# Output matmuls of a pair issued ahead of a later pair's scores, transposes behind them, in an encoder trunk

## The chip, the core and the metric

The kernel runs on one core of one Trainium2 chip, as one launch with everything in 32-bit floats. The metric is the device time of one execution in microseconds (us). Times of the kernel before: 1628.23, 1629.42 and 1628.72, median 1628.72.

The engines are named as the profile names them: PE (TensorE, matmuls), DVE (VectorE), ACT (ScalarE), POOL (GpSimd) and SP (SyncE, which only issues DMAs here). Each works through a queue of its own, in an order fixed when the program is built, and waits on semaphores for the others.

## The reference

Two sequences of 256 tokens with 1024 features go through two layers that share their weights between the sequences. Cut to what matters here:

```python
h = rmsnorm(x, attn_norm[l])
a_cols, b_cols, c_cols, d_cols, g_cols = split(h @ w_in[l])
o_a = diff_mixer(a_cols)     # 4 heads, two softmaxes of 32-row heads, their difference
o_b = natten_mixer(b_cols)   # 4 heads of 64, neighbourhood mask and a position bias b_rpb
o_c = mla_mixer(c_cols)      # low-rank queries and keys, 96 rows a head
o_d = gqa_mixer(d_cols)      # 4 query heads of 64, 2 key heads, rotary in two axes
merged = sum(sigmoid(g_cols_i) * (o_i @ w_branch[l, i]))
x = x + merged @ w_out[l]
x = x + conv_ffn(rmsnorm(x, ffn_norm[l]))      # gated, width 2816, 3-tap conv
...
y = rmsnorm(x, final_norm)                     # after both layers
```

In each mixer `softmax(q k^T) v` is taken per head over the 256 keys of the own sequence.

## The kernel before

**Pieces and units.** Both sequences lie side by side as T = 512 columns, the features on the partitions, so a projection is a sum of matmuls with a 128x128 weight block and 512 columns of activations. The weights are read once, in a fixed order, as pieces of mostly 128 x 1024 values (512 KB). SP loads piece by piece into three `raw` buffers (`load_piece`, L267). Each is split into a rounded high part and the rest (`split_piece`, L278): ACT writes `wh` (L288), then DVE the first half of `wl` (L291) and POOL the second (L292). Every product is three matmuls, `wh` by `xh`, `wh` by `xl` and `wl` by `xh` (`mm3`, L296 to L298), so that a piece of 8 blocks gives 24 matmuls. The work on one piece is a unit. The program's units follow the order of the pieces: queries and keys of mixer b (units 1 to 4, `psbq` and `psbk`), values of b (`psvb`), then mixers a, d and c, then gates `pg` with branch products `pb`, output projection, and the MLP. Projections land in four PSUM banks in turn; a bank comes free when its evacuation has read it.

**Side work.** Everything that isn't a projection is written as generators that are handed from unit to unit. Those of the diff and of the prediction:

- `pair_gen` (L811): attention of two heads for one sequence. Scores `sc` of the pair (L744; for mixers a, b and d interleaved on parts of the array, `scores_rows`), softmax of the first head, softmax of the second, then two groups of four transposes (`pt`, L787), each copied to SBUF by ACT as `ptr` (L793); then the output matmuls `po` (L842, four calls that the trace shows as eight matmuls; the two heads use the two halves of 64 columns of the array), and their evacuation. TLAG and PLAG are numbers of extra steps ahead of the transposes and ahead of `po`, for each mixer.
- `sq_gen` (L1154): the squares of x for the first normalisation, added up by `sq_acc` (squares on ACT; additions on DVE, L338).
- `norm_gen`: the statistics matmuls `st` (L344, columns of one element), then the mean square `ms` and a newton iteration for 1/sqrt on DVE (L306 to L352, ending in the copy `rs`), then four transposes that broadcast it (`rb`, L357), the copy `rsrow` (L372), and on POOL the rotary tables times that row (`cosr`, `sinr`, L379 and L380). Projections run on unnormalised x; their evacuation multiplies by `rsrow` (`bc`, L601, for `psbq` and `psbk`).
- `bias_gen` (L698): 16 DMAs of the position bias on SP's queue (L695), then on POOL four additions of the mask (L704).
- `lam_gen`: the scalars `lam` of mixer a on DVE (L1173 to L1179).

**Order.** The loop from L1185 goes over the units. At the start of a unit every active generator takes one step, in the order of priority and, within one, in the order in which they were added. Then come the unit's own matmuls, one more step of the generators (`vec(0)`, `vec(1)`) with the evacuations that are due, the split of the piece two units on, and the load of the piece five units on. `sq_gen` is added in unit 0 and yields twice; `norm_gen` and `bias_gen` are added in later units. What is written in this order then passes a scheduler of the framework, which fixes the order on each engine when the program is built: it may put an instruction past others on its engine. What stands in the program is therefore read from the order of the built program, not from the loop alone.

**Buffers in PSUM.** The banks are four for projections (two of the scores of mixer a take theirs there too), two for scores, one for the transposes `pt`, and one that `po`, `st` and `rb` share.

Of the kernel before, what the change touches and what calls it, by code (L numbers as in the profile page):

```python
# [32 lines left out]
GX = [(25, 29), (31, 32)]  # L33
GBR = {n: n - BLAG for n in range(BLAG, 30)} | {30: 29, 31: 30}
TLAG = {"a": 1, "b": 1, "c": 0, "d": 0}
PLAG = {"a": 2, "b": 0, "c": 1, "d": 2}
GAP = {"a": 3, "b": 2, "c": 2, "d": 3}
START = {"a": ("ak0", 7), "b": ("bk0", 4), "c": ("cv", 6), "d": ("vf1", 2)}
CLAG = 1
# [162 lines left out]
def trunk_kernel(ctx: ExitStack, tc: tile.TileContext, xt, wflat, gains, lams, rpb, consts, yt):  # L202
# [22 lines left out]
    def psum(nm, pool=pm):  # L225
        tag = {id(pm): "m", id(psx): "s", id(pst): "t", id(pso): "o"}[id(pool)]
        return pool.tile([128, T], F32, tag=tag, name=nm)
# [7 lines left out]
    def rows64(ap):  # L235
        return ap.rearrange("p (r c) -> p r c", c=64)
# [30 lines left out]
    def load_piece(i, parts=1):  # L267
        if i >= len(order):
            return
        n = _piece_cols(order[i][1])  # L270
        raw = wpool.tile([128, 1280], F32, tag="raw", name=f"raw{i}", bufs=RAW_BUFS)
        src = wflat[offs[i]:offs[i] + 128 * n].rearrange("(p n) -> p n", p=128)
        c = n // parts
        for q in range(parts):
            nc.sync.dma_start(out=raw[:, q * c:q * c + c], in_=src[:, q * c:q * c + c])
        raws[i] = raw
# [23 lines left out]
    def split(v, h, l, eng=None):  # L300
        S.activation(out=h, in_=v, func=AF.Copy)  # L301
        (eng or V).tensor_tensor(out=l, in0=v, in1=f(h), op=ALU.subtract)  # L302
# [132 lines left out]
    def build_layer(l):  # L435
# [271 lines left out]
        def heads(mix, j):  # L707
            if mix == "a":
                return [[(f"aq{j}", f"ak{j}", 32 * (2 * e + c), 32) for c in range(2)] for e in range(2)]
            if mix == "b":  # L710
                return [[(f"bq{j}", f"bk{j}", 64 * e, 64)] for e in range(2)]
            if mix == "c":
                return [[(f"cq{2 * j + e}", f"ck{2 * j + e}", 0, 96)] for e in range(2)]
            return [[(f"dq{j}", "dk", 64 * e, 64)] for e in range(2)]
# [3 lines left out]
        def scores(maps, b):  # L718
            out = []
            for qn, kn, p0, n in maps:  # L720
                ps = psum("sc", psx)
                (qh, ql), (kh, kl) = att[qn], att[kn]
                ks = slice(b * 256, b * 256 + 256)
                p = slice(p0, p0 + n)
                for qt in range(2):
                    qs = slice(b * 256 + qt * 128, b * 256 + qt * 128 + 128)
                    o = ps[:, qt * 256:qt * 256 + 256]
                    PE.matmul(o, lhsT=qh[p, qs], rhs=kh[p, ks], start=True, stop=False)
                    PE.matmul(o, lhsT=qh[p, qs], rhs=kl[p, ks], start=False, stop=False)
                    PE.matmul(o, lhsT=ql[p, qs], rhs=kh[p, ks], start=False, stop=True)  # L730
                out.append(ps)
            return out

        def scores_rows(maps, b):
            pss = [psum("sc", psx if i < 2 else pm) for i in range(len(maps))]
            ks = slice(b * 256, b * 256 + 256)
            for qt in range(2):
                qs = slice(b * 256 + qt * 128, b * 256 + qt * 128 + 128)
                for term in range(3):
                    for ps, (qn, kn, p0, n) in zip(pss, maps):  # L740
                        p = slice(p0, p0 + n)
                        q = att[qn][1 if term == 2 else 0]
                        k = att[kn][1 if term == 1 else 0]
                        PE.matmul(ps[:, qt * 256:qt * 256 + 256], lhsT=q[p, qs], rhs=k[p, ks],  # L744
                                  start=(term == 0), stop=(term == 2))
            return pss
# [36 lines left out]
        def trans(p):  # L783
            ps = psum("pt", pst)
            for kt in range(2):
                for qt in range(2):
                    PE.transpose(out=ps[:, kt * 256 + qt * 128:kt * 256 + qt * 128 + 128],  # L787
                                 in_=p[:, qt * 256 + kt * 128:qt * 256 + kt * 128 + 128], identity=ident)
            return ps

        def trans_evac(ps):
            t = t2("ptr")
            S.activation(out=t, in_=ps, func=AF.Copy)  # L793
            return t

        def v_of(mix, j, e, tt):
            if mix == "a":
                return vA[:, tt, (2 * j + e) * 64:(2 * j + e) * 64 + 64]
            if mix == "b":
                return vB[:, tt, (2 * j + e) * 64:(2 * j + e) * 64 + 64]  # L800
            if mix == "c":
                return vC[:, tt, (2 * j + e) * 64:(2 * j + e) * 64 + 64]
            return vD[:, tt, e * 64:e * 64 + 64]

        def o_tile(mix, j, part, dt):
            key = ("o", mix, j, part)
            if key not in att:
                att[key] = t2(f"o{mix}{j}{part}", dt)
            return att[key]

        def pair_gen(mix, b, j):  # L811
            hs = heads(mix, j)
            rows = mix in "abd"
            if rows:
                ss = scores_rows(hs[0] + hs[1], b)
                s0, s1 = ss[:len(ss) // 2], ss[len(ss) // 2:]
            else:
                s0 = scores(hs[0], b)
            yield
            p0 = softmax(mix, j, 0, s0)  # L820
            yield
            if not rows:
                s1 = scores(hs[1], b)
            yield
            p1 = softmax(mix, j, 1, s1)
            yield
            for _ in range(TLAG[mix]):
                yield
            t0 = trans(p0)
            yield  # L830
            pt0 = trans_evac(t0)
            yield
            t1 = trans(p1)
            yield
            pt1 = trans_evac(t1)
            yield
            for _ in range(PLAG[mix]):
                yield
            ops = psum("po", pso)
            for kt in range(2):  # L840
                for e, pt in ((0, pt0), (1, pt1)):
                    PE.matmul(ops[64 * e:64 * e + 64, :256], lhsT=v_of(mix, j, e, 2 * b + kt),  # L842
                              rhs=pt[:, kt * 256:kt * 256 + 256], start=(kt == 0), stop=(kt == 1))
            yield
            bs = slice(b * 256, b * 256 + 256)
            if mix == "a":
                S.activation(out=o_tile("a", j, "f", F32)[:, bs], in_=ops[:, :256], func=AF.Copy)
            else:
                h, lo = o_tile(mix, j, "h", F32R), o_tile(mix, j, "l", F32R)
                if mix == "b":  # L850
                    split(rows64(ops[:, :256])[:, :, ::-1], rows64(h[:, bs]), rows64(lo[:, bs]))
                else:
                    split(ops[:, :256], h[:, bs], lo[:, bs])
            yield
# [34 lines left out]
        def at(step, gen, pri=1):  # L889
            starts.setdefault(step, []).append((pri, gen))  # L890
# [198 lines left out]
        for mix in ORD:  # L1089
# [6 lines left out]
            if mix == "a":  # L1096
                at(s - GAP[mix] + 4 + (TLAG["a"] + PLAG["a"] + 1) // 2, a_norm_gen)
        tabs = row_tables()
# [83 lines left out]

    units[3]["side"].append((1, lam_gen))

    active, pending = [], []  # L1185
    for i, u in enumerate(units):
        active += [(pri, g()) for pri, g in u["side"]]
        active.sort(key=lambda a: a[0])
        live = []
        for pri, g in active:  # L1190
            if next(g, 1) is None:
                live.append((pri, g))
        active = live
        wh, wl = splits.pop(i)
        u["pe"](wh, wl)

        def vec(want):
            for a in list(active):
                if a[0] == want:
                    if next(a[1], 1) is not None:  # L1200
                        active.remove(a)

        vec(0)
        now = [e for e in pending if e[0] <= i]
        pending = [e for e in pending if e[0] > i]
        for _, e in now:
            e()
        vec(1)
        split_piece(i + LOOK)
        load_piece(i + LOOK + RAW_BUFS)  # L1210
        if u["now"] and u["evac"] is not None:
            u["evac"]()
        elif u["evac"] is not None:
            pending.append((max(i + 1, u["nb"]), u["evac"]))
# [58 lines left out]
```

## Time and profile before

| what | value |
|---|---|
| median of 3 runs | 1628.72 us |
| the profiled execution, its own time | 1629.04 us |
| its span in the trace | 1627.3 us |
| PE busy | 1610.2 us, 99% of the span, 8163 matmuls |
| DVE busy | 962.9 us, 59% |
| ACT busy | 620.5 us, 38% |
| POOL busy | 661.2 us, 41% |
| DMA | 146.84 MB on SP's queue, 26.8% of the 16 DMA engines' span |
| mean granted clock of PE | 0.995 of full speed |

The span is the part of the execution that the trace covers; the 1.7 us around it belong to the execution's own time. PE's busy share is that of its matmuls with modelled ends: they overlap, and where PE is never idle a stretch is read by the steps from one matmul's start to the next. In the chain that ended last PE holds 97%, DVE and ACT 1% each.

### The profile page before, as it was taken

How to read it: one execution, taken by the hardware profiler on the slowest of the kernel's cores; microseconds unless marked ns; L12 is line 12 of the kernel's file. 1: busy time of each engine (PE TensorE's matmuls, PEld its weight loads, DVE VectorE, ACT ScalarE, POOL GpSimd, SP SyncE). 2: the span in 40 equal slices, each digit the busy share in tenths (PEclk: the TensorE clock that was granted, in tenths of full speed). 3: DMA queues.
4: the chain of work that ended last, by engine and by line, in shares of the span. 5: the costliest groups of instructions: out<-in, count | busy, mean ns of one | idle time of the engine just before them, and what ended most of it. 6: DMA issues, size and time to landing. Idle time of an engine off the chain costs nothing.

```text
span 1627.3 us, 21327 instructions
## 1 busy us (share of the span) xinstructions
PE 1610.2 (99%) x8163; PEld 1336.7 (82%) x8163; DVE 962.9 (59%) x1580; ACT 620.5 (38%) x1107; POOL 661.2 (41%) x449
## 2 busy tenths in 40 slices
PE   8999999999999999999999999999999999999997
PEld 6898788888888888888888977888788888888886
DVE  7767485656876665633366665756468656665113
ACT  4446354333333333322234555434332333333221
POOL 4432223445534444444445231244455344444342
PEclk9999999999999999999999999999999999999999
DMA  6213122221322322223332222222222222322331
GB/s 220 101 53 98 56 98 82 81 78 59 116 91 91 104 95 98 90 95 105 102 105 85 67 88 72 82 86 76 81 78 104 92 95 99 104 91 86 105 96 64
DMA packets 50534, 149.25 MB, mean 92 GB/s; under 512 B 13184, under 2 KB 16128, under 8 KB 50432
## 3 DMA queue, kind: packets, MB, share of 16 engines
q1 hardware_dynamic: 49344, 146.84, 26.8%
q8 instruction: 64, 1.05, 0.3%
q10 hardware_dynamic: 1088, 1.05, 0.2%
q14 instruction: 38, 0.31, 0.1%
HBM read 145.77 MB, written 2.10 MB: 91 GB/s over the span
## 4 chain that ended last, share of the span: by engine, by line
PE 97%; DVE 1%; ACT 1%; issue 1%; DMA 0%; POOL 0%; SPq 0%; POOLq 0%; ACTq 0%
PE pf L296 10%; PE pf L297 10%; PE pf L298 10%; PE pg L296 7%; PE pg L297 7%; PE pg L298 7%; PE pfo L296 5%; PE pfo L297 5%; PE pfo L298 5%; PE po L842 2%; PE pt L787 2%; PE pb L298 2%; PE pwo L296 2%; PE pb L297 2%; PE pb L296 2%; PE pwo L298 2%
## 5 line engine op out<-in xcount | busy, mean ns | idle before, releaser
L292 POOL TENSOR_TENSOR wl<-raw,wh 128x512 fp32r<-128x512 f32 (+4 forms) x264 | 454.4, 1723 | 567.6 <-ACT wh L288 466.6
L288 ACT ACTIVATE wh<-raw 128x1024 fp32r<-128x1024 f32 (+5 forms) x264 | 281.6, 1067 | 437.4 <-PE pfo L297 128.2
L291 DVE TENSOR_TENSOR wl<-raw,wh 128x512 fp32r<-128x512 f32 (+4 forms) x262 | 258.9, 988 | 227.6 <-ACT wh L288 209.8
L296 PE MATMUL pf<-xh,wh 128*128 128x512 f32 x704 | 274.3, 390 | 0.0
L298 PE MATMUL pf<-xh,wl 128*128 128x512 f32 x704 | 273.9, 389 | 0.0
L297 PE MATMUL pf<-xl,wh 128*128 128x512 f32 x704 | 273.9, 389 | 0.0
L296 PE MATMUL pg<-xh,wh 128*128 128x512 f32 x512 | 203.4, 397 | 0.4
L297 PE MATMUL pg<-xl,wh 128*128 128x512 f32 x512 | 199.7, 390 | 0.0
L298 PE MATMUL pg<-xh,wl 128*128 128x512 f32 x512 | 199.7, 390 | 0.0
L296 PEld LDWEIGHTS pf<-xh,wh 128*128 128x128 f32 x704 | 132.2, 188 | 27.4
L298 PEld LDWEIGHTS pf<-xh,wl 128*128 128x128 f32 x704 | 132.2, 188 | 27.4
L297 PEld LDWEIGHTS pf<-xl,wh 128*128 128x128 f32 x704 | 132.2, 188 | 27.3
L296 PE MATMUL pfo<-ah,wh 128*128 128x512 f32 (+1 forms) x374 | 141.1, 377 | 0.0
L297 PE MATMUL pfo<-al,wh 128*128 128x512 f32 (+1 forms) x374 | 140.8, 376 | 0.0
L298 PE MATMUL pfo<-ah,wl 128*128 128x512 f32 (+1 forms) x374 | 140.8, 376 | 0.0
L911 POOL TENSOR_TENSOR mg<-mg,gz 128x512 f32<-128x512 f32 x48 | 64.4, 1346 | 165.5 <-DVE gz L910 165.5
L302 POOL TENSOR_TENSOR al<-fc,ah 128x512 fp32r<-128x512 f32 x44 | 57.8, 1315 | 178.9 <-ACT ah L301 178.9
L296 PEld LDWEIGHTS pg<-xh,wh 128*128 128x128 f32 x512 | 96.2, 188 | 23.4 <-issue 1.3
L298 PEld LDWEIGHTS pg<-xh,wl 128*128 128x128 f32 x512 | 96.1, 188 | 20.7
L297 PEld LDWEIGHTS pg<-xl,wh 128*128 128x128 f32 x512 | 96.3, 188 | 18.4
L932 ACT ACTIVATE gz<-gz 128x512 f32<-128x512 f32 x64 | 40.3, 630 | 133.9 <-DVE gz L931 133.8
L767 ACT ACTIVATE pr<-sc,mx 128x256 f32<-128x256 f32 x128 | 59.0, 471 | 73.5 <-DVE mx L762 73.5
(386 smaller groups left out, 2841.5 us busy)
## 6 DMA issues: line engine op xcount, KB each, us to landing
raw<-in_w_dram SPq DMA_DIRECT2D x158, 512.0 KB, 3.2
raw<-in_w_dram SPq DMA_DIRECT2D x58, 640.0 KB, 3.8
raw<-in_w_dram SPq DMA_DIRECT2D x32, 448.0 KB, 3.2
raw<-in_w_dram SPq DMA_DIRECT2D x4, 576.0 KB, 3.3
bias<-in_rpb_dram SPq DMA_DIRECT2D x32, 64.0 KB, 3.0
xall<-in_xt_dram SPq DMA_DIRECT2D x3, 512.0 KB, 7.4
raw<-in_w_dram SPq DMA_DIRECT2D x4, 256.0 KB, 4.8
out_dram<-y SPq DMA_DIRECT2D x4, 256.0 KB, 2.4
```

Of the source, the lines that this page charges most:

```text
L288: S.activation(out=wh[:, a:b], in_=raw[:, a:b], func=AF.Copy)
L291: V.tensor_tensor(out=wl[:, a:c], in0=raw[:, a:c], in1=f(wh[:, a:c]), op=ALU.subtract)
L292: G.tensor_tensor(out=wl[:, c:b], in0=raw[:, c:b], in1=f(wh[:, c:b]), op=ALU.subtract)
L296: PE.matmul(ps, lhsT=wh, rhs=xh, start=first, stop=False)
L297: PE.matmul(ps, lhsT=wh, rhs=xl, start=False, stop=False)
L298: PE.matmul(ps, lhsT=wl, rhs=xh, start=False, stop=last)
L302: (eng or V).tensor_tensor(out=l, in0=v, in1=f(h), op=ALU.subtract)
L767: S.activation(out=p[:, qt * 256:qt * 256 + 256], in_=src[c][:, qt * 256:qt * 256 + 256], func=AF.Exp, scale=sc, bias=mx[:, i:i + 1], accu ...
L787: PE.transpose(out=ps[:, kt * 256 + qt * 128:kt * 256 + qt * 128 + 128], in_=p[:, qt * 256 + kt * 128:qt * 256 + kt * 128 + 128], identity ...
L842: PE.matmul(ops[64 * e:64 * e + 64, :256], lhsT=v_of(mix, j, e, 2 * b + kt), rhs=pt[:, kt * 256:kt * 256 + 256], start=(kt == 0), stop=(kt ...
L911: G.tensor_tensor(out=m, in0=m, in1=z, op=ALU.add)
L932: S.activation(out=z, in_=z, func=AF.Tanh, scale=0.5)
```

## The change

`PLAG` gets other values, 0 now meaning that `po` comes in the very next step. The last step ahead of `po` yields the word "po" instead of nothing. The loop keeps with each generator the word that it yielded last ("new" for one that has just been added), and at the start of a unit it lets those go first whose word is "po", then the new ones, then all others. The second step within a unit goes by priority and age, as before.

```diff
--- before.py
+++ after.py
@@ -33,7 +33,7 @@
 GX = [(25, 29), (31, 32)]
 GBR = {n: n - BLAG for n in range(BLAG, 30)} | {30: 29, 31: 30}
 TLAG = {"a": 1, "b": 1, "c": 0, "d": 0}
-PLAG = {"a": 2, "b": 0, "c": 1, "d": 2}
+PLAG = {"a": 3, "b": 3, "c": 0, "d": 3}
 GAP = {"a": 3, "b": 2, "c": 2, "d": 3}
 START = {"a": ("ak0", 7), "b": ("bk0", 4), "c": ("cv", 6), "d": ("vf1", 2)}
 CLAG = 1
@@ -833,9 +833,11 @@
             t1 = trans(p1)
             yield
             pt1 = trans_evac(t1)
-            yield
-            for _ in range(PLAG[mix]):
+            yield None if PLAG[mix] else "po"
+            for _ in range(PLAG[mix] - 1):
                 yield
+            if PLAG[mix]:
+                yield "po"
             ops = psum("po", pso)
             for kt in range(2):
                 for e, pt in ((0, pt0), (1, pt1)):
@@ -1182,22 +1184,22 @@
 
     units[3]["side"].append((1, lam_gen))
 
-    active, pending = [], []
+    active, pending, DONE = [], [], object()
     for i, u in enumerate(units):
-        active += [(pri, g()) for pri, g in u["side"]]
+        active += [[pri, g(), "new"] for pri, g in u["side"]]
         active.sort(key=lambda a: a[0])
-        live = []
-        for pri, g in active:
-            if next(g, 1) is None:
-                live.append((pri, g))
-        active = live
+        for a in sorted(active, key=lambda a: {"po": 0, "new": 1}.get(a[2], 2)):
+            a[2] = next(a[1], DONE)
+            if a[2] is DONE:
+                active.remove(a)
         wh, wl = splits.pop(i)
         u["pe"](wh, wl)
 
         def vec(want):
             for a in list(active):
                 if a[0] == want:
-                    if next(a[1], 1) is not None:
+                    a[2] = next(a[1], DONE)
+                    if a[2] is DONE:
                         active.remove(a)
 
         vec(0)
```

What the built programs have on PE near their start, as a difference (lines with - of the kernel before, with + of the changed one). `psbq` and `psbk` are projections of mixer b, `psvb` its values in unit 5, `sq_172` is the sum of squares, `rs` the 1/sqrt of the mean square:

```order
 L296 MATMUL psbq_288<-xh_160,wh_211 128x512
-L344 MATMUL st<-cst,sq_172 128x1 x4
 L297 MATMUL psbq_288<-xl_161,wh_211 128x512
...
 L296 MATMUL psbk_344<-xh_134,wh_276 128x512
-L357 MATMUL rb<-cst,rs 128x128 x4
 L297 MATMUL psbk_344<-xl_135,wh_276 128x512
...
 L298 MATMUL psbk_344<-xh_168,wl_277 128x512
+L344 MATMUL st<-cst,sq_172 128x1 x4
+L357 MATMUL rb<-cst,rs 128x128 x4
 L454 MATMUL psvb<-wh_332,xh_122 128x256
```

`st` moved from the third unit to the end of the fourth, and `rb` from the fourth unit to right behind `st`; no matmul stands between the two now. The second layer's `st` and `rb` keep 24 matmuls between them.

On DVE, the same stretch of the program. `wl_277`, `wl_333` and `wl_412` are the halves of pieces 3, 4 and 5 that DVE splits; the other rows add a square to the sum:

```order
 L338 TENSOR_TENSOR sq_172<-sq_172,sq_208 128x512
-L338 TENSOR_TENSOR sq_172<-sq_172,sq_218 128x512
-L338 TENSOR_TENSOR sq_172<-sq_172,sq_221 128x512
 L291 TENSOR_TENSOR wl_277<-raw_132,wh_276 128x512
-L338 TENSOR_TENSOR sq_172<-sq_172,sq_224 128x512
 L291 TENSOR_TENSOR wl_333<-raw_150,wh_332 128x512
+L291 TENSOR_TENSOR wl_412<-raw_216,wh_411 128x512
+L338 TENSOR_TENSOR sq_172<-sq_172,sq_238 128x512
+L338 TENSOR_TENSOR sq_172<-sq_172,sq_241 128x512
+L338 TENSOR_TENSOR sq_172<-sq_172,sq_244 128x512
 L349 TENSOR_SCALAR ms<-st 128x4
```

The last three additions went behind the splits of pieces 3 to 5; the ACT squares that they read went behind ACT's part of piece 5 in the same way. On POOL the four bias additions stand in a row right behind its half of piece 5, where two stood there and two behind `cosr` and `sinr`.

On PE at the start of a gate unit of layer 0, with a pair of mixer d under way; in the kernel before:

```order
L298 MATMUL pb<-oa1h,wl_2751 128x512
L787 MATMUL pt<-cst,pr 128x128 x4
L744 MATMUL sc<-dkh,dq1h 128x256 x2
L744 MATMUL sc<-dkl,dq1h 128x256 x2
L744 MATMUL sc<-dkh,dq1l 128x256 x2
```

and in the changed kernel (`vD` are the values of mixer d, `pr` the probabilities):

```order
L298 MATMUL pb<-oa1h,wl_2751 128x512
L844 MATMUL po<-ptr,vD 64x256 x4
L744 MATMUL sc<-dkh,dq1h 128x256 x2
L744 MATMUL sc<-dkl,dq1h 128x256 x2
L744 MATMUL sc<-dkh,dq1l 128x256 x2
L744 MATMUL sc<-dkh,dq1h 128x256 x2
L744 MATMUL sc<-dkl,dq1h 128x256 x2
L744 MATMUL sc<-dkh,dq1l 128x256 x2
L787 MATMUL pt<-cst,pr 128x128 x4
```

The output matmuls of an older pair now stand directly ahead of the scores, and the transposes that stood ahead of the scores come behind them. (A row with x4 or x2 stands for that many instructions that read alike.)

## Rows read from the trace of the kernel before

**Rows 1.** Head of the page and its section 1, busy times.

```profile
span 1627.3 us, 21327 instructions
...
PE 1610.2 (99%) x8163; PEld 1336.7 (82%) x8163; DVE 962.9 (59%) x1580; ACT 620.5 (38%) x1107; POOL 661.2 (41%) x449
```

**Rows 2.** Stretches: length, busy us of PE, PEld, DVE, ACT, POOL; clock, DMA, GB/s.

```profile
5.90:9.30 3.40, 0.05 (x1) 0.00 (x0) 0.50 (x1) 1.88 (x4) 1.88 (x2) 0.83 0.98 342
9.30:14.90 5.60, 5.56 (x12) 3.97 (x13) 5.53 (x9) 3.06 (x5) 1.64 (x2) 0.50 1.04 410
40.00:780.00 740.00, 739.70 (x3751) 613.46 (x3748) 451.55 (x720) 289.77 (x525) 301.46 (x202) 1.00 0.26 88
```

**Rows 3.** Time line of PE, 73 to 76.5: start, length, line, out<-in, shapes.

```profile
73.21 0.39 PE L297 MATMUL psak<-xl,wh 128*128 128x512 f32 x1
73.44 0.39 PE L298 MATMUL psak<-xh,wl 128*128 128x512 f32 x1
73.75 1.08 PE L842 MATMUL po<-ptr,vB 128*64 128x256 f32 x8
...
75.36 0.38 PE L744 MATMUL sc<-bk1h,bq1h 64*128 64x256 f32 x1
75.58 0.28 PE L744 MATMUL sc<-bk1l,bq1h 64*128 64x256 f32 x1
75.70 0.28 PE L744 MATMUL sc<-bk1h,bq1l 64*128 64x256 f32 x1
...
76.05 0.28 PE L744 MATMUL sc<-bk1h,bq1l 64*128 64x256 f32 x1
76.26 0.38 PE L454 MATMUL psvd<-wh,xh 128*128 128x256 f32 x1
76.48 0.28 PE L455 MATMUL psvd<-wl,xh 128*128 128x256 f32 x1
```

**Rows 4.** Time line of PE, 26.3 to 35.3.

```profile
26.39 1.02 PE L344 MATMUL st<-cst,sq 128*128 128x1 f32 x8
27.27 0.48 PE L297 MATMUL psbq<-xl,wh 128*128 128x512 f32 x1
...
30.15 0.62 PE L357 MATMUL rb<-cst,rs 128*128 128x128 f32 x4
...
35.17 0.28 PE L454 MATMUL psvb<-wh,xh 128*128 128x256 f32 x1
```

**Rows 5.** Time line of ACT, high part of piece 5.

```profile
29.23 1.06 ACT L288 ACTIVATE wh<-raw 128x1024 fp32r<-128x1024 f32 x1 [5.47 <-DVE ny L313]
```

**Rows 6.** Time line of DVE, operations that read SBUF alone.

```profile
23.30 0.69 DVE L338 TENSOR_TENSOR sq<-sq,sq 128x512 f32<-128x512 f32 x1
...
30.49 1.70 DVE L291 TENSOR_TENSOR wl<-raw,wh 128x512 fp32r<-128x512 f32 x1
...
32.12 1.25 DVE L1177 TENSOR_TENSOR lam<-lp 128x1 f32<-128x1 f32 x1
```

**Rows 7.** Time line of POOL, 30.3 to 34.6.

```profile
30.36 1.29 POOL L292 TENSOR_TENSOR wl<-raw,wh 128x512 fp32r<-128x512 f32 x1 [5.22 <-ACT wh L288]
31.61 1.74 POOL L704 TENSOR_TENSOR bias<-bias,cst 128x512 f32<-128x512 f32 x1
33.31 1.28 POOL L704 TENSOR_TENSOR bias<-bias,cst 128x512 f32<-128x512 f32 x1
```

**Rows 8.** Time line of DVE, from `rs` to `bc`.

```profile
29.83 0.17 DVE L352 COPY rs<-ny 128x4 f32<-128x4 f32 x1
...
33.54 0.68 DVE L372 COPY rsrow<-rb 128x512 f32<-128x512 f32 x1
34.26 0.69 DVE L601 TENSOR_TENSOR bc<-psbq,rsrow 128x512 f32<-128x512 f32 x1
```

**Rows 9.** Time line of ACT, 104 to 107, a split and a copy of transposes.

```profile
104.78 1.05 ACT L288 ACTIVATE wh<-raw 128x1024 fp32r<-128x1024 f32 x1
...
106.04 0.60 ACT L793 ACTIVATE ptr<-pt 128x512 f32<-128x512 f32 x1
```

## The prediction

> **What bounds the kernel now.** I read the page first, then the busy times by stretch, then the time line of TensorE (PE) at two places, and last the time lines of VectorE (DVE), GpSimd (POOL) and ScalarE (ACT) in the first 36 us. PE is busy 1610.2 of 1627.3 us [rows 1], and between 40 and 780 us it lacks only 0.30 of 740 us [rows 2]. So whatever makes the PE queue longer, or makes PE wait, lands in the time one for one, and a wait cannot be repaid later: there is almost no idle time to absorb it. A gain has to come out of the PE queue itself. What is to be seen in the PE rows is the step from one start to the next, not the printed durations, which overlap.
>
> **Part 1: what changes among po, sc and pt on PE.** The array works in three shapes here: full (projections, gates, transposes pt), 128x64 (output matmuls po) and 64x128 or 32x128 (scores sc of mixers a, b, d). Scores of mixer c read 96 rows and behave as full. Each change of shape costs time that belongs to no matmul. In one passage of before [rows 3]: plain matmuls of 512 columns step by 0.23; the step into po is 0.31, and another 0.05 goes behind the first pair, so entering po costs about 0.14. Into scores, the first two are 0.22 apart where later ones step 0.12, and about 0.10 goes ahead of the first: 0.20. Out of scores 0.21 and 0.22 stand where 0.12 is normal: 0.19. Out of po into transposes costs some 0.16, since the passage from 73.44 to 76.48 (3.04) holds 0.23 + 4 x 0.216 (po pairs) + 4 x 0.109 (transposes) + 6 x 0.118 + 0.12 = 2.36 of plain steps, and 0.68 is left for the four changes: 0.17 each.
>
> The order F, po, pt, sc, F has four changes; F, po, sc, pt, F has three. That is the good side, 0.17 us wherever it happens. I counted it over the whole order of the changed program: 134 changes of shape before, 124 after. Entries into scores from full fall from 27 to 15, direct steps po to sc rise from 4 to 20, but scores now leave into full 33 times instead of 27, and some po groups are still cut in two by the scheduler (a single po matmul, four transposes, then three). Ten changes at 0.17 are -1.7. Against that two more po steps stand alone (70 against 68, 0.43 each, a pair that no longer runs side by side: +0.86) and four more score steps (164 against 160, 0.12 each: +0.47). Net -0.4 us. If every one of the 20 direct steps were a saved change and the cuts cost nothing it would be 20 x 0.17 = -3.4; if the cuts cost double, +1. I take -0.4, the count.
>
> **Part 2: what moves at the start of the program.** The new loop advances generators that have just been added ahead of those under way. In the second unit that puts the bias loads ahead of the last three squares of the first normalisation, and the scheduler then places these squares, and the DVE additions that follow, behind the split of weight piece 5 (the order rows of the change). So the statistics matmuls st, which in before stand inside the third unit, come after the fourth, and the broadcast rb follows st at once with nothing between. I work this out on the times of before.
>
> *When st can start.* Without st (0.88 us, from 26.39 to 27.27) and rb, PE runs the 32 matmuls left of units 3 and 4 without a stop: 26.39 + 32 x 0.227 = 33.6 [rows 3, 4]. Are its inputs there? ACT splits piece 5 when unit 3 has freed the buffer: at 29.23 in before, about one us sooner now, 28.2 to 29.2 [rows 5]; the three squares (half that size, 0.53 each) follow by 30.8. Then come DVE's low half of piece 5 and three additions of 128x512, 0.69 each when alone [rows 6]. But POOL now has, in the same stretch, its half of piece 5 and all four bias additions in a row. In before a DVE operation with SBUF operands that starts beside a POOL operation takes 1.70 instead of about 0.68, and a 128x1 one takes 1.25: each ends where the POOL operation that was running ends [rows 6, 7]. So the additions alternate with POOL: the first ends near 31.6, the second 33.3, the third 35.0, and st starts at 35.1 (33.6 if they did not collide).
>
> The Trainium skill says the same thing as a rule (SBUF — State Buffer, section "SBUF: two separate sides"): the port pair that VectorE and GpSimd share is an exclusive lock held for a whole instruction, and the one that comes second blocks fully. By that rule three additions among POOL's additions are one wait each; without it the sum below is 2.7 smaller, which is a rival.
>
> *From st to rb.* In before the copy that rb needs ends at 30.00, and rb starts at 30.15 [rows 4, 8], 2.88 behind the end of st's steps at 27.27. Twelve matmuls cover this now. In the change nothing covers it: +2.88 of idle PE. One more bias addition (1.2) stands in the middle of the newton chain of small DVE operations: st 35.1 to 36.0, rb at 39.8, done at 40.4.
>
> *From rb to the next matmul.* Four PSUM banks serve the projections, and units 1 to 4 fill all four; psvb of unit 5 needs the first back, which the row copy rsrow and the product bc give (33.54 and 34.26, 0.68 and 0.69) [rows 8]. In before this was done at 34.95 and psvb came at 35.17 without waiting [rows 4]. Now: 40.4 + 0.7 (rsrow) + 0.3 (four small lam operations, now behind rsrow) + 0.7 (bc) = 42.2. PE restarts 7.0 us later than before. Behind it on DVE wait the split of piece 6 and the bq0 and bk0 products, beside POOL's two table products, which start from rsrow as well; the scores of the first pair would start 8 us later than before by the same lengths. I take +8.0 for the stall.
>
> *The clock.* In before PE stood nearly still from 5.9 to 9.3, and from 9.3 to 14.9 the granted clock was 0.50, 1.2 GHz [rows 2]. The new gap, 34 to 42 with 1.3 us of small work in it, is longer. 5.6 us at half speed would lose up to 2.8, but PE waits for DVE in the same stretch anyway, so I take +0.5 and keep 0 to 2.8 for the range.
>
> The second layer keeps its order (st, 24 matmuls, rb), so this is paid once.
>
> **Part 3: new waits behind the moved transposes.** Two transpose groups of a pair share one PSUM bank. In before they are often a unit apart or have po and sc between; in the change twice per layer the second follows the first with only 1.0 to 1.5 us between. Its ACT copy (0.60) can be queued behind a weight split of 1.05 [rows 9]. By those rows the second group would wait 0.45 in one place and 0.76 in the other, 2.4 us over two layers; nothing if ACT is free. I take half, +1.2. Later po evacuations feed branches that run many units on; the last po of each layer is not later than before. SP's queue keeps its order of loads and bias loads in the first layer.
>
> **Sum.** -0.4 + 8.0 + 0.5 + 1.2 = +9.3 us. The profiled execution took 1629.04 (its span is 1627.3); 1629.04 + 9.3 = 1638.3. It lies 0.3 above the median 1628.72, so the forecast is 1638.0.
>
> **Rivals.**
> *No collisions.* st starts at 33.6 when PE gets there, newton runs unhindered, and psvb starts near 39.9: +4.7 instead of +7.0, no clock loss, little after it: 1628.7 - 0.4 + 4.7 + 0.6 = 1633.6. For it: DVE can win the first turn, and products that read PSUM ran beside POOL at full speed (bc, 0.69, beside the bias addition at 33.31) [rows 7, 8]. Against: additions between SBUF tiles did not.
> *Everything at its upper end.* Clock at half for all of 5.6 us (+2.8), the transposes' waits in full (+2.4), one more POOL collision in front of bc (+1.2): 1628.7 - 0.4 + 8.0 + 6.4 = 1642.7.
> *The other side: the saved changes of shape decide and the start costs nothing.* The place is the unit starts of mixers a and d, the price 0.17 a place. It decides if the stall at the start stays under 1 us, which needs psvb not to wait for the row: 1628.7 - 3.4 + 0.5 = 1625.8. For it: the direct steps exist in the order. Against: st and rb stand side by side in it, and the chain between them is 2.9 us of dependent operations.
> *No change to be seen.* A partial stall, around 3 us, that the reorder pays back in part: 1628.7 + 2 = 1630.7. It needs the newton chain hidden by something, and I see nothing in the PE queue there.
>
> **How the numbers follow.** Forecast as worked out (8 to 11 us more) 0.55; no collisions 0.24; upper end 0.11; a small or hidden stall 0.06; faster 0.04. A measurement of this kernel can tell 0.2% (3.3 us) from no change. The two ends of the stall are +4.7 and about +14; the range 1632.5 to 1642.5 holds the first two cases and part of the third. Slower by over 0.2%: 0.55 + 0.24 + 0.11 = 0.90; within: 0.06; faster: 0.04.
>
> **What would show it.** In the profile after: st near 35, rb near 40 and psvb near 42, with two PE waits there, on the newton chain and on bc; POOL's four bias additions in a row with DVE's sq additions stretched to 1.6 beside them; a second stretch of granted clock below 1.0 in the first 50 us. The scores right behind po should show the first step 0.31 (po to sc) and no transposes between. From 50 us on the two traces should run side by side, apart by 8 to 10 us, with no further gap over 1 us. I am wrong if psvb starts before 38, if the distance between the traces shrinks or grows by more than 3 us after 50, or if changes of shape cost visibly less between po and sc than between po and transposes.

## The result and the profile after

The changed kernel takes 1641.85 us (median of 6 runs, 1641.12 to 1643.25), the kernel before 1628.88 (6 runs, 1628.23 to 1629.42): ratio 1.0082, 95% interval 1.0072 to 1.0092, so 13.0 us more. The forecast was 1638.0, 9.3 more, with a range up to 1642.5. At the start direction, mechanism and size came out as worked out, some 8 us. Behind it came 4.5 us, where 0.8 had been put down.

Head and busy times of the profile after, which answer to [rows 1]:

```profile
span 1640.4 us, 21314 instructions
...
PE 1613.3 (98%) x8163; PEld 1341.4 (82%) x8163; DVE 959.1 (58%) x1580; ACT 621.2 (38%) x1107; POOL 666.6 (41%) x449
```

The span grew by 13.1 and PE's busy time by 3.1, most of it matmuls at the lower clock (below). The other ten are idle time of PE.

**Where it goes.** Both programs have the same projections in the same order, so the start of one and the same matmul in both traces gives the distance between them. Worked out from the time lines of PE:

| matmul | before, start | after | squares first | start only | b at 0 |
|---|---|---|---|---|---|
| `psbk` of unit 2, 12th | 18.59 | +0.43 | -1.08 | -0.91 | -0.64 |
| `psvb`, 30th | 40.64 | +8.81 | -0.26 | +7.41 | -0.04 |
| `psvd`, first (76.26 in [rows 3]) | 76.26 | +9.91 | +0.83 | +7.44 | -0.01 |
| `psva`, first | 124.28 | +12.45 | +3.38 | +7.43 | -0.02 |
| `pg`, 673rd (layer 0) | 373.94 | +11.37 | +2.31 | +7.42 | -0.80 |
| `psvd`, first of layer 1 | 876.98 | +12.22 | +3.03 | +7.33 | -1.01 |
| `pg`, 1441st (layer 1) | 1174.90 | +13.42 | +4.29 | +7.35 | -2.07 |

(The last three columns are experiments, below.) The first row shows how far apart two executions can stand before PE's order has changed: the first `psbk` starts at 9.34 in before, 9.63 in after and 8.98 with the squares first, by when the first loads land, and the granted clock rises from 0.50 to 1.00 at 14.9, 15.5 and 12.7. Counted from that row there are two things in the column of after, +8.4 by 41 us and +4.6 behind it, together the 13.0 of the medians. The 4.6 come in places that are the same in both layers, with about 1 us given back between `psva` and `pg`.

**The start.** PE, answering to [rows 3, 4]:

```profile
33.75 0.39 PE L298 MATMUL psbk<-xh,wl 128*128 128x512 f32 x1
35.53 1.02 PE L344 MATMUL st<-cst,sq 128*128 128x1 f32 x8 [1.39 <-issue]
40.13 1.09 PE L357 MATMUL rb<-cst,rs 128*128 128x128 f32 x4 [3.57 <-DVE rs L352]
43.01 0.55 PE L454 MATMUL psvb<-wh,xh 128*128 128x256 f32 x1 [1.80 <-DVE bc L601]
43.36 0.42 PE L455 MATMUL psvb<-wl,xh 128*128 128x256 f32 x1
...
46.30 0.28 PE L454 MATMUL psvb<-wh,xh 128*128 128x256 f32 x1
46.41 0.28 PE L455 MATMUL psvb<-wl,xh 128*128 128x256 f32 x1
```

The prediction had st at 35.1, rb at 39.8 and psvb at 42.2; it is 35.5, 40.1 and 43.0, and the three waits (1.39 for the last addition of squares, which the profile books as issue; 3.57 on the newton chain; 1.80 on bc) are those of its working (its list of signs had only the last two). DVE and then POOL in this stretch, answering to [rows 6 to 8]:

```profile
30.27 5.17 DVE L338 TENSOR_TENSOR sq<-sq,sq 128x512 f32<-128x512 f32 x3
...
36.79 1.01 DVE L306 TENSOR_SCALAR ny<-ms 128x4 int32<-128x4 int32 x1
...
41.25 0.69 DVE L372 COPY rsrow<-rb 128x512 f32<-128x512 f32 x1 [0.70 <-PE rb L357]
...
42.19 0.68 DVE L601 TENSOR_TENSOR bc<-psbq,rsrow 128x512 f32<-128x512 f32 x1
```

```profile
29.70 1.80 POOL L292 TENSOR_TENSOR wl<-raw,wh 128x512 fp32r<-128x512 f32 x1 [3.65 <-ACT wh L288]
31.47 6.30 POOL L704 TENSOR_TENSOR bias<-bias,cst 128x512 f32<-128x512 f32 x4
```

Three additions take 5.17 beside POOL's row of four, and one newton step on four columns takes 1.01 where its neighbours take 0.16. Between the end of rb at 40.57 and rsrow at 41.25 DVE waits 0.70. The clock, answering to [rows 2] (same columns):

```profile
33.75:43.01 9.26, 2.50 (x14) 1.71 (x13) 6.88 (x28) 1.26 (x3) 5.01 (x4) 0.80 0.28 112
43.01:46.30 3.29, 3.29 (x16) 3.29 (x16) 3.11 (x3) 0.66 (x2) 3.29 (x3) 0.51 0.00 0
```

PE stands still for most of the first stretch; in the second it is busy throughout at a granted clock of 0.51, the 1.2 GHz level, and psvb steps by 0.21 instead of 0.12. Its first sixteen take 1.5 us longer than in before for that reason. Half a microsecond of it comes back, because the scores among them find their inputs ready, where before had a wait of 0.44: between the first psvb and the 30th the distance grows from 7.84 to 8.81.

**Behind the start.** The same stretch of the program in after and in before, busy and idle (columns as in [rows 2]):

```profile
54.00:1213.00 1159.00, 1153.48 (x6053) 958.43 (x6052) 694.40 (x1204) 464.32 (x905) 462.99 (x312) 1.00 0.25 86
```

```profile
45.00:1200.00 1155.00, 1153.24 (x6055) 956.19 (x6055) 700.13 (x1207) 463.84 (x905) 459.63 (x312) 1.00 0.26 87
```

PE is busy 0.24 us longer, and idle 5.52 against 1.76. What it waits for there (us in total, times, longest), after and then before:

```profile
PE pt L787 <- ACT ptr L793: 2.0, 4, 0.6
PE po L844 <- DVE ob1l L302: 1.4, 2, 0.7
PE rb L357 <- DVE rs L352: 0.9, 1, 0.9
PE sc L744 <- DVE cf L519: 0.6, 2, 0.3
PE ab L357 <- DVE od0l L302: 0.4, 2, 0.2
```

```profile
PE rb L357 <- DVE rs L352: 1.0, 1, 1.0
PE po L842 <- ACT ptr L793: 0.2, 1, 0.2
```

Four kinds of wait are new, 4.4 us together, each once or twice a layer.

These idle times begin at the modelled ends of the matmuls ahead, which overlap what follows. By the steps from one start to the next a wait costs more. Worked out from the time lines, from the 30th psvb to the 1441st pg: from each step at which the profile shows a wait, subtract the median of like steps without one. What is left comes to 6.7 us in after and 1.4 in before (pt 2.3, po 1.5, sc 0.9, ab 0.8 are new). All else is 0.6 us shorter in after. So the new waits cost about 5.2, the new order of shapes gives back about 0.6, and the two make the 4.6 of the table.

Two places show what three of the four have in common. First the second transposes of a pair of mixer b, on PE and on ACT:

```profile
115.70 0.28 PE L744 MATMUL sc<-ak0h,aq0l 32*128 32x256 f32 x4
116.60 0.66 PE L787 MATMUL pt<-cst,sb 128*128 128x128 f32 x4 [0.62 <-ACT ptr L793]
```

```profile
115.01 1.05 ACT L288 ACTIVATE wh<-raw 128x1024 fp32r<-128x1024 f32 x1
115.96 0.59 ACT L793 ACTIVATE ptr<-pt 128x512 f32<-128x512 f32 x1
```

The first transposes had ended at 115.1; the copy that frees their bank starts when ACT's weight split ends. Then po, whose bank the evacuation of the po before it must free, on PE, ACT and DVE:

```profile
135.40 1.08 PE L844 MATMUL po<-ptr,vB 128*64 128x256 f32 x8 [0.72 <-DVE ob1l L302]
```

```profile
133.14 1.05 ACT L288 ACTIVATE wh<-raw 128x1024 fp32r<-128x1024 f32 x1
134.09 0.38 ACT L301 ACTIVATE ob1h<-po 128x256 fp32r<-128x256 f32 x1
```

```profile
134.23 0.69 DVE L291 TENSOR_TENSOR wl<-raw,wh 128x512 fp32r<-128x512 f32 x1 [0.45 <-ACT wh L288]
134.84 0.42 DVE L302 TENSOR_TENSOR ob1l<-po,ob1h 128x256 fp32r<-128x256 f32 x1
```

The weight split comes first twice here, 1.05 on ACT and 0.69 on DVE, and only then is po's bank read out. (The matmuls that filled it had ended at 118.3. The evacuation has its place in ACT's order far behind them, and the split is only what stands last ahead of it.) The wait of ab is of this kind too: od0h stands behind a split of 1.27 on ACT, od0l behind one of 0.83 on DVE. The wait of the scores is not. Their bank, which psvf filled by 132.5, is read by fsq on ACT and then by the copy cf on DVE at 133.29, and it is fsq that cf waits for, not a split.

### The profile page after: what moved, and what is told of

Its sections match the earlier page's. It is cut to its first block, busy times and chain, and to the rows that moved or that the text cites. A ratio compares the mean times of both kernels' runs of the same rounds, so it can differ in the third digit from the quotient of the medians.

```text
span 1640.4 us, 21314 instructions
## 1 busy us (share of the span) xinstructions
PE 1613.3 (98%) x8163; PEld 1341.4 (82%) x8163; DVE 959.1 (58%) x1580; ACT 621.2 (38%) x1107; POOL 666.6 (41%) x449
## 3 DMA queue, kind: packets, MB, share of 16 engines
q1 hardware_dynamic: 49344, 146.84, 26.3%
q8 instruction: 64, 1.05, 0.3%
q10 hardware_dynamic: 1088, 1.05, 0.2%
## 4 chain that ended last, share of the span: by engine, by line
PE 97%; ACT 1%; DVE 1%; issue 1%; DMA 0%; POOL 0%; SPq 0%; POOLq 0%; ACTq 0%
PE pf L296 10%; PE pf L298 10%; PE pf L297 10%; PE pg L296 7%; PE pg L297 7%; PE pg L298 7%; PE pfo L297 5%; PE pfo L296 5%; PE pfo L298 5%; PE po L844 2%; PE pwo L296 2%; PE pt L787 2%; PE pwo L298 2%; PE pwo L297 2%; PE pb L298 2%; PE pb L297 2%
## 5 line engine op out<-in xcount | busy, mean ns | idle before, releaser
L291 DVE TENSOR_TENSOR wl<-raw,wh 128x512 fp32r<-128x512 f32 (+4 forms) x262 | 254.9, 973 | 221.6 <-ACT wh L288 211.9
L933 DVE TENSOR_TENSOR gz<-pg,rsrow 128x512 f32<-128x512 f32 x64 | 44.1, 689 | 75.7 <-PE pg L298 70.0
```

The lines of the kernel that those rows point to most:

```text
L291: V.tensor_tensor(out=wl[:, a:c], in0=raw[:, a:c], in1=f(wh[:, a:c]), op=ALU.subtract)
L933: V.tensor_tensor(out=z, in0=pg, in1=st["row"], op=ALU.mult)
```

## The experiments

Theory A is that start and waits are two separate costs; B that all comes from the start; C the prediction's sizes. Theories of later runs are their own, as said in what was expected of each. Each kernel was timed beside the kernel before on the same chip.

**Squares first** (1633.18, 7 runs; before 1628.64; ratio 1.0027 [1.0017, 1.0038]). The changed kernel with the old order at the start; the word "po" lets the squares step first:

```diff
             if d in (2, 4):
-                yield
-        yield
+                yield "po"
+        yield "po"
```

> The changed kernel, with the squares of the first normalisation stepping ahead of the bias loads again; the order on PE differs from the changed kernel only in st and rb, which go back to units 3 and 4. Theory A (start and later waits are two separate costs): the start gives back 9.0 us, what is lost behind 50 us (4.1 us by the distance between the two traces) stays: 1641.85 - 9.0 = 1632.9, with the same four PE waits per layer on the copies behind a weight split. Theory B (all of it comes from the start, the distance that grows later is a consequence of the shift): about 1629, no waits of 0.4 us or more in mixer b. Theory C (as predicted, the later part is worth -0.4 + 1.2): 1629.7.

A holds: 1632.9 was expected. The waits of mixers b, c and d are all there (2.0, 1.4, 0.6 and 0.4 as above), and in the table the distance grows by 4.55 from 41 us on, as in after by 4.61. B is out, and so is C's 1629.7.

**Start only** (1636.48, 5 runs; ratio 1.0048 [1.0035, 1.0061]). The kernel before, in which unit 1 lets the bias loads go first:

```diff
         active.sort(key=lambda a: a[0])
+        if i == 1:
+            active = active[-1:] + active[:-1]
...
-        active = live
+        active = sorted(live, key=lambda a: a[0])
```

> The kernel before, with only the bias loads stepping ahead of the last squares in unit 1: PE, DVE, ACT and POOL have the changed kernel's order up to unit 5 and the order of before behind it. Theory A: 1628.88 + 9.0 = 1637.9, the distance to before constant at 9.0 from 50 us to the end. Theory B: 1641.9, the distance grows by 4 us behind 50 as in the changed kernel. Theory C: 1637.4 (8.5 predicted for the start).

7.84 us (5.7 to 9.9 by the interval), which fits C's 8.5 and A's 9.0 and not B, and the distance stays at 7.3 to 7.4 from 41 us to the end. With the 4.54 of the run before it makes 12.4 of the 13.0 measured; the 0.6 left is inside the intervals.

**No mask additions** (1638.72, 5 runs; 3.1 us less than the changed kernel). POOL's four additions of layer 0 are left out:

```diff
-                G.tensor_tensor(out=b3, in0=b3, in1=m, op=ALU.add)
+                if l:
+                    G.tensor_tensor(out=b3, in0=b3, in1=m, op=ALU.add)
```

> The changed kernel without the four mask additions on POOL in layer 0 (the mask of mixer b is left out there, nothing else). If DVE's additions of squares and the first newton step are stretched by these POOL operations (5.17 us for three, 1.01 for one of four columns), st starts at 34.0, when PE gets there, instead of 35.5, rb 2.4 us sooner, and the whole takes 1641.85 - 2.4 = 1639.4. If the additions wait for the squares of ACT or for the split of piece 5 and not for POOL, nothing moves: 1641.9.

DVE's rows and then PE's:

```profile
29.34 3.38 DVE L338 TENSOR_TENSOR sq<-sq,sq 128x512 f32<-128x512 f32 x3
...
34.24 0.17 DVE L306 TENSOR_SCALAR ny<-ms 128x4 int32<-128x4 int32 x1
```

```profile
33.20 0.81 PE L344 MATMUL st<-cst,sq 128*128 128x1 f32 x6
...
39.14 0.55 PE L454 MATMUL psvb<-wh,xh 128*128 128x256 f32 x1 [1.79 <-DVE bc L601]
```

The additions take 3.38 instead of 5.17 (the first still stands beside POOL's split), the newton step 0.17 instead of 1.01, st starts as soon as PE gets there, and, counted from the last `psbk` ahead of st, rb comes 2.5 sooner (2.4 expected) and psvb 3.0. Then the low clock lasts over 22 psvb and not 15, and by the 30th 1.8 are left of it; in the medians it is 3.1, and the two intervals just meet. So the collisions are real, and worth some 2 to 3 of the start's 8; the rule that the prediction cites from the Trainium skill (SBUF — State Buffer, section "SBUF: two separate sides") agrees with these rows.

**Matmuls of no use in the gaps**, four of 128x512 behind st (1641.20, 5 runs) and then two (1640.36, 5 runs), both with 16 transposes behind rb. They are added to the changed kernel; their results are not read. The run with two has `range(2)` in the first block. Each of these matmuls shows as two rows.

```diff
         main_stats(ps)
+        if wait == 2:
+            fp = psum("fill", psx)
+            for k in range(4):
+                PE.matmul(fp, lhsT=st["accs"][0][:, :128], rhs=st["accs"][0], start=(k == 0), stop=(k == 3))
...
         row_bcast(pb, lambda t: rs[:, t:t + 1].to_broadcast([128, 128]))
+        if wait == 2:
+            fp = psum("fill", psx)
+            for k in range(4):
+                row_bcast(fp, lambda t: rs[:, t:t + 1].to_broadcast([128, 128]))
```

> The changed kernel with matmuls of no use in its two gaps at the start: four of 128x512 behind st and sixteen transposes behind rb, both into a bank for scores that nobody reads. If the granted clock falls because PE stands still there, the clock stays up, psvb's first sixteen matmuls step by 0.12 instead of 0.21 and rb takes 0.6 instead of 1.1: 1641.85 - 1.7 = 1640.2. If the clock falls whatever PE does there: 1641.9. If the four run past 40.1 and hold rb back: more than 1641.9.

> As the run with matmuls of no use in the gaps at the start, with two of 128x512 and not four behind st, which end ahead of rs. Eight rows took 5.38 there, so four take about 2.8 and end near 39.1, 0.7 ahead of rs. If the clock stays up: rb at 40.0 as in the changed kernel, psvb by 42.7, its steps 0.12 instead of 0.21 for sixteen matmuls: 1641.85 - 1.7 = 1640.2. If the clock falls in the 0.9 us between them and rs: 1641.9.

PE with four, and then with two, and the same stretch with four and with two (columns as in [rows 2]):

```profile
36.25 5.38 PE L367 MATMUL fill<-sq 128*128 128x512 f32 x8
41.46 0.60 PE L357 MATMUL rb<-cst,rs 128*128 128x128 f32 x4
```

```profile
35.67 1.96 PE L367 MATMUL fill<-sq 128*128 128x512 f32 x4
39.37 0.62 PE L357 MATMUL rb<-cst,rs 128*128 128x128 f32 x4 [1.74 <-DVE rs L352]
...
41.98 0.28 PE L463 MATMUL psvb<-wl,xh 128*128 128x256 f32 x1
42.10 0.28 PE L464 MATMUL psvb<-wh,xl 128*128 128x256 f32 x1
...
45.64 0.38 PE L752 MATMUL sc<-bk0h,bq0h 64*128 64x256 f32 x2 [0.98 <-ACT bk0h L301]
```

```profile
33.70:43.00 9.30, 7.91 (x33) 4.60 (x32) 6.43 (x26) 1.15 (x2) 5.26 (x5) 0.82 0.27 109
33.70:43.00 9.30, 6.43 (x42) 4.97 (x43) 7.49 (x28) 1.79 (x3) 5.53 (x5) 1.00 0.26 106
```

With four the granted clock fell all the same: it was 0.50 from 36.5 to 39.8, while PE worked on them without a stop. So they took 5.38 for eight rows, where the other run took 1.96 for four. They ran past the end of the newton chain (rs was there at 39.81) and held rb back by 1.5, which ate what the full clock behind it gave. With two the granted clock is 1.00 throughout, rb takes 0.62 instead of 1.09 and psvb steps by 0.12 from the start: 1.5 us less than the changed kernel in the median, 1.7 expected, though the two intervals overlap. In the traces the stretch from the last `psbk` before st to the 30th psvb is 0.8 us shorter than in after; part of what the clock gave went into the wait of 0.98, in which the scores stand now that psvb is faster. That work in the gap keeps the clock up is not shown: it fell in one of the two runs with work there, and there is one trace of each.

**PLAG of mixer b at 2** (1628.06, 11 runs; ratio 0.9998 [0.9989, 1.0007]) **and at 0** (1626.80, 11 runs; ratio 0.9989 [0.9980, 0.9998]). Both on top of squares first; the second has `"b": 0` where the first has `"b": 2`:

```diff
-PLAG = {"a": 3, "b": 3, "c": 0, "d": 3}
+PLAG = {"a": 3, "b": 2, "c": 0, "d": 3}
```

> As the run with the squares first, and PLAG of mixer b at 2 instead of 3. By the count of the order no po or score group is cut now, and plain steps and changes of shape together come to 2.5 us less than in before. Theory A1 (the waits come from two transpose groups close together with a copy behind a weight split, and stay whatever PLAG is): 1628.9 - 2.5 + 3.9 = 1630.3. Theory A2 (the waits in mixer b come from PLAG 3, by which po is late and its bank too): 1628.9 - 2.5 + 0.8 = 1627.2, faster than before. If changes of shape and cuts cost nothing: 1632.9, as without this edit.

> As the run with the squares first, with PLAG of mixer b back at 0, its value before; mixers a, c and d keep the new values. By the count of the order plain steps and changes of shape come to 2.7 us less than in before, 0.2 less than with PLAG 2 for b. If the wait of a transpose group in mixer b (0.45 us a layer, the second group behind a copy that stands behind a weight split) goes with its PLAG: 1628.6 - 2.7 + 0.8 (the wait of ab, 0.4 a layer, stays) = 1626.7, faster than before by 0.12%. If the waits of mixer b stay or go elsewhere: 1628, no change.

With 2, waits of mixer b remain (0.8 of the 2.0 on ptr; that of po is gone, and 0.4 for a projection's bank stands instead), and it lies between A1 and A2: no change against before. With 0 the waits in the same stretch are

```profile
PE rb L357 <- DVE rs L352: 1.0, 1, 1.0
PE ab L357 <- DVE od0l L302: 0.4, 2, 0.2
```

and the time is 1.5 us under before, 1626.7 expected. It beats both kernels. By the steps, worked out as above, all that is not a wait is 2.6 us shorter than in before with 2 and 2.5 with 0, near the counts of 2.5 and 2.7, but only 0.6 with 3. So of the 6.6 us between the trace with 0 and that of squares first, 4.6 are waits and 2.0 are groups that the scheduler cuts. What the change keeps here (the new PLAG of a, c and d, and the loop's order for all four mixers) pays by its changes of shape; it costs by PLAG 3 in mixer b and at the start. Which of a, c and d pays was not tried apart.

**Copies of mixer b's transposes on DVE** (1644.92, 4 runs; ratio 1.0100 [1.0086, 1.0114]), on top of squares first:

```diff
-            S.activation(out=t, in_=ps, func=AF.Copy)
+            if mix == "b":
+                V.tensor_copy(out=t, in_=ps)
+            else:
+                S.activation(out=t, in_=ps, func=AF.Copy)
...
-            pt0 = trans_evac(t0)
+            pt0 = trans_evac(t0, mix)
```

> As the run with the squares first (PLAG b 3), but DVE and not ACT copies the transposes of mixer b to SBUF, so that these copies no longer stand behind ACT's weight split. Theory A (the waits of the second transposes and of po in mixer b are that queue): the two waits of transposes on a copy (0.45 and 0.69 a layer) go, 2.3 us over both layers, and the order has 0.7 us less in changes of shape: 1633.2 - 3.0 = 1630.2. Rival (DVE is as late, since its half of the split and the softmax stand there): the waits are there with DVE as the engine waited for, 1633 or more.

```profile
PE pt L787 <- DVE ptr L794: 7.6, 4, 2.7
```

The rival came true, only larger: DVE's queue is worse (2.7 us in one place), and it says nothing on ACT's split. So the split itself was shortened.

**Half of the split on DVE** for two pieces a layer (1632.76, 9 runs; ratio 1.0027 [1.0017, 1.0037]), on top of squares first:

```diff
-            S.activation(out=wh[:, a:b], in_=raw[:, a:b], func=AF.Copy)
             c = a if pool_only else (a + b) // 2
+            if order[i][1] in ("ve0", "va0"):
+                S.activation(out=wh[:, a:c], in_=raw[:, a:c], func=AF.Copy)
+                V.tensor_copy(out=wh[:, c:b], in_=raw[:, c:b])
+            else:
+                S.activation(out=wh[:, a:b], in_=raw[:, a:b], func=AF.Copy)
```

> As the run with the squares first (PLAG b 3, 1633.2), but for the two weight pieces a layer whose split stands on ACT ahead of the late copies, DVE makes half of the high part, so that ACT's instruction is half as long. Theory A (a transpose group waits for its bank, the bank for ACT's copy, the copy for ACT's split): the copy comes 0.55 sooner, the waits of 0.45 and 0.69 a layer become 0 and 0.14, 2.0 us over both layers; the order has 0.75 us more in plain steps and changes of shape, so 1633.2 - 1.3 = 1631.9. Rival (the copy waits for something else, or the bank is not what the transposes wait for): the two waits stay as they are, 1634.

```profile
PE pt L791 <- ACT ptr L797: 0.8, 4, 0.2
```

The waits on these copies fall from 2.0 to 0.8, and the others stay as they were (1.4, 0.6, 0.4): the split ahead of the copy is what makes these transposes wait. For po and ab the same is read from the rows and not shown by a run. The whole gained only 0.4, inside the noise: by the steps the waits are 1.4 shorter and all else is 1.1 longer, where 0.75 was expected, since the scheduler cut another po group a layer (six rows, four transposes, then two).

## Why the prediction was right, and where its size was off

- **The start: +8.5 forecast, 7.8 by the run with it alone** and 8.4 in the trace of after. The order of causes (squares late, nothing between st and rb, the bank waiting for bc) and the three times were right within 0.8 us. The collisions of DVE and POOL, 2.7 in the text, measured 1.8 to 3.1. The rival "no collisions" is out by the run without mask additions.
- **Readings in the start that were off.** A DVE operation does not always end where the POOL operation beside it ends. The 128x1 one does (33.37 and 33.35), but the split of [rows 6] ends at 32.19, behind POOL's 31.65, and the additions in after end at 32.06, 33.75 and 35.43, each 0.55 behind a POOL operation; st came 0.4 later by that. From st to rb the terms in the text add up to 40.1, where it says 39.8; 40.13 was measured. The 0.70 for which DVE waits from rb to rsrow stood at nothing.
- **That the start's sum fits so well is partly luck.** Scores that come another 1.0 later were in it, and in after they cost nothing, while the clock was put at +0.5 and cost 1.5 in the first sixteen psvb. The two overlap: where the clock stayed up, the scores waited 0.98. Net the clock was worth 0.8 in the traces, 1.5 in medians whose intervals overlap.
- **Changes of shape and cuts: -0.4 forecast, about -0.6** by the steps (PE's busy time, +0.24, has the matmuls' overlap in it). The count of the order was right, and the rival that expected -3.4 is out.
- **The step that failed is the term of new waits, +1.2, which measured 4.2 by the waits that the profile lists and 5.2 by the steps.** Its first part, the second transposes behind a copy, was worked out as 0.45 and 0.76 a place, 2.4 in full; listed are 0.4 to 0.6 and 2.0 in full, by the steps 2.3. I halved it on the ground that ACT might be free; both times in both layers it was not. Its second part was missing: the prediction looked at the bank of pt, and not at the one that po, ab and st share. Moving po changes when that bank is read out, and the evacuation goes through ACT and DVE, behind a weight split on each: listed are 1.4 for po and 0.4 for ab. And 0.6 for scores of mixer a that take a bank from the projections'. The sentence that later po evacuations feed branches many units on was true and not the point: PE needs the bank sooner than the branch needs the result.
- **"With no further gap over 1 us" behind 50 us** was kept for single waits (0.72 the longest new one), but the distance did grow by 4.6, more than the 3 us that the prediction set as its own bound. By that sign of its own it was wrong behind the start.
- **The time inside the range owes something to chance.** It comes near the 1642.7 of "everything at its upper end", and not by that way: the clock did not cost 2.8, no further POOL collision stood in front of bc, and the waits cost more than the 2.4 put down as their full size.

What stays open: the two halves measured apart make 12.4 of 13.0, inside the intervals; why the clock fell with four matmuls of no use and not with two; and what the splits ahead of po and ab alone are worth, which no run took away.

## What to carry to other kernels

Where one engine is busy 99% of the time, ask of each moved instruction which buffer it takes, who must read that out, and what stands ahead of that reader on its own queue; here a weight split of 1.05 to 1.27 us stood ahead in three of four kinds of wait, and all four cost some 5 us, where the whole new order of shapes gave back 0.6. A rule that lets new work go first acts at the program's start as well, where nothing is there to cover it: 8 of the 13 us came from an effect in unit 1 that has nothing to do with the outputs and scores it was written for. A reordering rule is best tried mixer by mixer: with mixer b's PLAG and the start as before, it is 0.11% faster.

## What the runs showed of the hardware that was not expected

- The granted clock stayed at 1.00 over a stretch of 9.3 us in which PE was busy 6.4, and was 0.51 behind one of the same length in which it was busy 2.5; but it also fell to 0.50 within one in which PE was busy 7.9 (four matmuls of no use). Where it stayed up, the kernel took 0.8 us less in the traces and 1.5 in medians whose intervals overlap.
- A DVE instruction on four columns took 1.01 beside a POOL addition, and 0.17 without it: it ended with the POOL addition, at 37.80 and 37.77. A short operation can wait for the whole rest of a long one.
- Executions of programs whose order on PE agrees up to that point stood up to 1.5 us apart at 19 us, by when the first loads land and when the granted clock rises; distances between single traces are to be counted from behind such a point, or taken from medians.
